# A two-block transformer on one core: memory keys ahead of the neighbourhood output product, and the modulation steps in another place

## The chip, the cores and the metric

The kernel runs on one core of one Trainium2 chip. The metric is device time in microseconds (us) of one execution. Before the change three runs gave 3050.26, 3059.8 and 3065.61 us; their median, 3059.8 us, is the number that the change is measured against.

## What is computed

The first block takes 512 tokens of 1024 features, normalizes them to `h` and projects them by one wide matrix `w_in`. Three branches follow, each gated by a sigmoid of its own part of that projection:

```python
rq, rk, rv, rg, nq, nk, nv, xq, gate_logits = jnp.split(h @ w_in[l], split_points, axis=-1)
y_ret = _retention_branch(rq, rk, rv, rg, ...)                          # 4 heads, decay both ways, group norm
y_na = _neighbourhood_attention(nq, nk, nv, na_rpb[l]) @ w_na_o[l]      # 8 heads, 8 x 16 windows
y_xa = _memory_cross_attention(xq, _rmsnorm(mem, g_mem[l]), w_mem_kv[l]) @ w_xa_o[l]   # 4 heads, 256 rows
x = x + (g_ret * y_ret + g_na * y_na + g_xa * y_xa) @ w_out[l]
x = x + _hierarchical_moe(...)
```

The second block is two layers of attention and feed-forward, whose norms are modulated by vectors that depend on one condition row alone:

```python
mod = (silu_c @ w_ada[l] + b_ada[l])[:, None, :]      # 1024 x 6144, two layers: 48 MB of weights
```

This last product, called `ada` in the kernel, needs nothing from the first block. The kernel computes it in small steps beside the first block's work.

## The kernel before

**Products.** A float32 product is three products of rounded halves, hi·hi, lo·hi and hi·lo (`mm3`, lines 99 to 101). Weights come in chunks of 1 MB, [128, 2048]. A chunk is loaded into a place called `raw` by a DMA on SyncE's queue (line 70), copied to `whi` by ScalarE (line 81), and `wlo` is the difference, made by VectorE (line 82). There are three places for each of `raw`, `whi` and `wlo`. `W` makes a pair where it is needed, `ahead` makes it earlier.

**The modulation in steps.** `ada()` is a generator of 48 steps. A step loads 1 MB of `w_ada` into a `raw` place (line 1299) and multiplies it by the condition on TensorE, four products with 32 rows of output (line 1301). Every eighth step ends a part: ScalarE copies the sums to `adar` (line 1305), TensorE turns them by four 128x128 products, VectorE copies them to `mod` (line 1310); the next part begins with the bias, `b_ada`, which also takes a `raw` place (lines 1294 and 1296). The sums lie in one bank of PSUM that is used again by every part. `bg(n)` takes n steps.

**Stages of the first block**, with the time at which each ends in the trace: retention with its gates (222 us), its output product `branch_out` (316), neighbourhood projections (391), neighbourhood heads (450), output product of two groups of columns (485), memory keys and values (518), output product of the other two groups (553), projection of the memory queries (577), memory heads (610), output product (685), then `w_out`, the router and the experts.

- `retention` (stages `queries`, `values`, `scores` for two pairs of heads, then four gate projections, then the transposed rows `yTh`, `yTl` from line 94 and 95). `proj_b` makes each projection of 256 columns and ends with one `bg()` step.
- `na_table`, in the retention, writes the table of position biases to DRAM, `rpb_d`, by 16 DMAs of 192 KB on the Pool engine's queue (line 536).
- `branch_out` has four groups of 256 columns, each with a gate chunk of `w_in` through `proj_a` and then the `bo` product; before group 2 of the neighbourhood's it calls `memory_keys`.
- `pairs` runs an attention as a pipeline over pairs of query tiles: scores `xs` or `ns`, exponentials, turned probabilities `prt`, values `xpo` or `npo`. It takes one `bg()` step per two pairs of the neighbourhood's 16, and one per pair of the memory's 8.

**What sets the order.** A scheduler at build time puts every instruction into a fixed order on its engine and gives out places of a pool as they come free. At run time an engine waits at the head of its list. A load that needs a `raw` place waits on SyncE's queue until the last reader of that place is done, and later loads of that queue wait behind it.

Of the kernel before, what the change touches and what calls it, by code (L numbers as in the profile page):

```python
# [8 lines left out]
F = mybir.dt.float32  # L9
# [3 lines left out]
OP = mybir.AluOpType  # L13
# [10 lines left out]
# columns of the vector pack, in blocks of 128 features  # L24
# [8 lines left out]
# groups of 256 columns of the second block's input projection: name, first column  # L33
# [4 lines left out]
class Kern:  # L38
    def __init__(self, tc, ins, outs, stop=None):
        self.tc = tc  # L40
        self.nc = tc.nc
        self.i = ins
        self.o = outs
        self.stop = stop
        self.es = ExitStack()
        self.early = {}

# [6 lines left out]
    def W(self, ap, n=2048, k=None, steps=1, pin=False, eng=None):  # L54
        """Weight chunk [128, n] of float32 from DRAM as an exact pair of float32r tiles."""
        key = ap.tensor.name, ap.offset
        if key in self.early:
            return self.early.pop(key)
        return self.pair(self.raw(ap, n), n, k, steps, pin, eng)

    def ahead(self, *chunks):
        """Loads weight chunks (name, index, k) before their use; W finds them then."""
# [10 lines left out]
    def pair(self, raw, n=2048, k=None, steps=1, pin=False, eng=None):  # L73
        """pin: not before what the engines have to do first, though it may seem ready."""
# [12 lines left out]
    def split(self, hi, lo, src, scale=None, bias=None):  # L87
        """hi + lo = src (times scale), both float32r."""
# [15 lines left out]
    def psum(self, mm, big=0, words=1024, own=()):  # L104
        """Banks of PSUM: mm of one bank, big of several."""
# [16 lines left out]
    def rows6(self, name, dtype=F):  # L122
        """[128, 6, 1024]: six tiles of rows, or what else takes their place."""
        return self.yp.tile([128, 6, 1024], dtype, name=name, tag="rows", bufs=1)
# [12 lines left out]
    def bcast_rows(self, ap, n, parts=128):  # L137
        """DRAM row of n elements seen by all partitions."""
        return bass.AP(tensor=ap.tensor, offset=ap.offset, ap=[[0, parts], [1, n]])

    def rinv(self, ss, n, count, eps, name):
        """1/sqrt(ss/count + eps) for a [128, n] tile: a first guess from the bits of the float, three Newton steps.
        With -r for the guess, (v r^2 - 3) r is 2 of the next one, and so on: -1, 2, -16, 8192 of them; v is 8192^2 of its own."""
# [33 lines left out]
    def transpose_rows(self, rows, nt, dst, evac):  # L177
        """rows: list of [128, 1024] tiles; evac(kt, t0, n, psum [128, n*128])."""
# [25 lines left out]
    # =====================================================================  # L204
# [30 lines left out]
    def b1_norm(self):  # L235
        """Loads the rows and the first weights; first_norm(t) and first_turn(t) then make the part of h of tile t."""
        nc = self.nc
        # products of nothing, that start the tensor engine's clock
# [36 lines left out]
    def first_norm(self, t):  # L275
        """Norms the row tiles from t on that share a step: 0, 1, or 2 and 3."""
# [23 lines left out]
    def w_in(self, g):  # L300
        """Columns 256*g.. of w_in, all of K."""
        return self.W(self.i["w_in"][g, 0], k=8)

    def proj_b(self, g, evac, after=lambda t: None, before=()):
        """Tokens on partitions: out[tok, 256 columns of group g]."""
# [10 lines left out]
        self.bg()  # L316

    def proj_a(self, g, evac):
        """Columns on partitions: out[128 columns, 512 tokens]."""
# [17 lines left out]
    def retention(self):  # L337
# [6 lines left out]
        y = rp.tile([128, 4, 1024], F, name="y")              # [tok, tile, 4 heads of 256]  # L344
# [3 lines left out]
        def queries(c):  # L348
            """q and k of the heads 2c, 2c + 1: [128, hi or lo, head, tok]"""
# [34 lines left out]
        def scores(hd):  # L384
            # decay by the distance of the tokens: E[p, i - 128 j + 384] for tile j of the keys
# [15 lines left out]
        def outputs(hd):  # L401
# [4 lines left out]
            for i in range(4):  # L406
# [6 lines left out]
                # group norm over the head's 256 values  # L413
# [9 lines left out]
        # log sigmoid of the decays: min(x, 0) - log1p(exp(-|x|)), log1p by its atanh series  # L423
# [23 lines left out]
        nc.sync.dma_start(diff, self.i["posdiff"])  # L447
        values(0)
# [16 lines left out]
        # silu of the gate projection  # L465
        for j in range(4):
# [7 lines left out]
            self.proj_b(8 + j, evac)  # L474
        yT = [[self.s8("yTh", [4, 512]) for _ in range(2)], [self.s8("yTl", [4, 512]) for _ in range(2)]]
# [11 lines left out]
    def branch_rows(self):  # L487
        """Where the rows of an attention branch are collected: [tok, tile, 512]."""
        return self.mix[:, 4:6].rearrange("p a (b c) -> p (a b) c", b=2)

    def branch_out(self, yT, nk, wname, gate_group, first=False, middle=lambda: None):
        """mix^T += sigmoid(gate^T) * (w^T y^T), features on partitions."""
        nc = self.nc
        nw = 2048 // nk                       # columns of w per chunk
        w = None
        for g in range(4):
            if g == 2:
                middle()
            if g * 256 % nw == 0:
                w = self.W(self.i[wname][g * 256 // nw, 0], k=nk)  # L500

            def evac(f, p, g=g, w=w):
                mx = self.mixT[:, 2 * g + f]
                gt = self.t5("gate")
                nc.scalar.activation(gt, p, AF.Tanh, scale=0.5)
                nc.vector.tensor_scalar(gt, gt, 1.0, 0.5, op0=OP.add, op1=OP.mult)
                py = self.mm("bo")
# [9 lines left out]
            self.proj_a(gate_group + g, evac)  # L517

# [1 line left out]
    def na_table(self):  # L520
        nc = self.nc
        # relative position bias, expanded: E[qr, h, x, kr] = rpb[h, kr - qr + 7, x - 16], x = kc - qc + 31
# [7 lines left out]
        # per query column qq of a tile, the 32 columns of its key window, for the three tile types  # L530
        # (window starts 16, 8 and 0 columns before the tile): [qq, qr, h, type, 256]
# [6 lines left out]
    def neighbourhood(self):  # L538
# [5 lines left out]
        T = {}  # L544
# [13 lines left out]
        starts = (256, 192, 64, 0)               # key windows of the query tiles 3, 2, 1, 0  # L558
# [34 lines left out]
        self.pairs(16, scores, values, ("w_na_o", (0, 0), 4), ("w_in", (24, 0), 8), ("w_in", (25, 0), 8))  # L593
# [4 lines left out]
        oT = self.rows_to_T(o[:, ::-1])  # L598
        self.branch_out(oT, 4, "w_na_o", 24, middle=lambda: self.memory_keys(rows))

    def exps(self, out, s, m, scale):
        """out = exp(scale * (s - max)) for two tiles of queries [128, 2, 256]; returns 1 / row sums."""
# [10 lines left out]
    def pairs(self, n, scores, values, *chunks):  # L613
        """n pairs of query tiles: scores(i) -> probabilities [128, 2, 256], 1 / sums; values(i, turned, 1 / sums);
        chunks: weights that are needed next."""
# [3 lines left out]
        for i in range(n + 1):  # L619
# [17 lines left out]
            if i % 2 or n == 8:  # L637
                self.bg()
# [11 lines left out]
    def memory_rows(self):  # L650
        """Normed rows of the memory."""
# [14 lines left out]
    def memory_keys(self, rows):  # L666
        """Keys and values of the memory."""
# [25 lines left out]
    def memory_attention(self):  # L693
# [29 lines left out]
        self.pairs(8, scores, values, ("w_xa_o", (0, 0), 4), ("w_in", (28, 0), 8), ("w_in", (29, 0), 8))  # L723
# [7 lines left out]
    def b1_out(self, *stages):  # L731
        """stages: what follows for each tile of rows; the sums of squares of its parts are in self.xss."""
# [39 lines left out]
    # =====================================================================  # L772
    def moe(self):
# [21 lines left out]
        # normed rows, to DRAM for the gathers and transposed for the router  # L795
# [37 lines left out]
        # group: maximum of the softmax, first one on ties  # L833
# [45 lines left out]
        # slots: rank of the token among those of its expert, 512 slots per expert  # L879
# [20 lines left out]
        for k, w in ((0, w1), (1, w2)):  # L900
            # rank r and first slot 512 e of the token's k-th expert
# [10 lines left out]
            # the last expert's rows are not gathered  # L912
# [13 lines left out]
            # the rest: slot 512 e + r - CAP  # L926
# [1325 lines left out]
```

## Time and profile before

| what | value |
| --- | --- |
| runs | 3050.26, 3059.8, 3065.61 us, median 3059.8 |
| span of the profiled execution (its own time is not listed apart from the span) | 3055.9 us |
| median less span | 3.9 us |
| TensorE busy | 2907.7 us, 95% |
| VectorE, ScalarE, Pool busy | 1784.5, 1296.3, 483.3 us |
| DMA | 399.78 MB, 131 GB/s over the span |

TensorE is busy nearly all the time, so what can change is where it waits, and how long it runs at the lower of its two clocks after it has waited. The granted clock is given as a share of the full 2.4 GHz: 0.50 is 1.2 GHz. A wait is listed with what ended it. Line numbers are those of the kernel before; in the kernel after, lines past the first few are moved by one or more (the load is line 71, the split 82 and 83, the products 100 to 102, the modulation's load 1322 and product 1324).

### The profile page before, as it was taken

To read this page: it belongs to the slowest core of one execution; us is meant where nothing else is said; L and a number is where in the kernel's file an instruction comes from. 1 tells how busy PE (TensorE), PEld (TensorE's weight loads), DVE (VectorE), ACT (ScalarE), POOL (GpSimd) and SP (SyncE) were. 2 spreads that over 40 slices of the span, in tenths; PEclk is the share of its full clock that TensorE was granted. 3 is DMA by queue.
4 is the path that set the end of the run, shared out by engine and by line. 5 is a ranking of instruction groups with operands and counts; after the bars stand their busy time and mean duration, and the time that the engine had idled before them with its cause. 6 is when DMAs were issued, how large, how long until landed. Compare 5 with 4: busy or idle time off the path is not lost. (4 is left out here: it accounts for less than half of the span.)

```text
span 3055.9 us, 44719 instructions
## 1 busy us (share of the span) xinstructions
PE 2907.7 (95%) x17896; PEld 2473.1 (81%) x17896; DVE 1784.5 (58%) x3187; ACT 1296.3 (42%) x2275; POOL 483.3 (16%) x478
## 2 busy tenths in 40 slices
PE   8999999999899979899998999999898999899998
PEld 6997777679788869787688888888798776788887
DVE  6652254346688876788747242434665886644445
ACT  3232243324577754597645121211342876432222
POOL 2200010001110042255312000000310543100001
PEclk9999999999899989999999999999999999899999
DMA  5443464446799862510023121212143300322221
GB/s 197 153 140 138 143 234 152 183 155 242 267 392 378 312 225 75 179 27 19 1 90 128 59 71 54 78 48 83 62 138 98 96 20 1 125 110 96 97 97 69
DMA packets 130084, 399.78 MB, mean 131 GB/s; under 512 B 62199, under 2 KB 74887, under 8 KB 93128
## 3 DMA queue, kind: packets, MB, share of 16 engines
q1 hardware_dynamic: 116206, 350.04, 31.9%
q0 software_dynamic: 13520, 46.55, 4.6%
q8 instruction: 143, 2.34, 0.3%
q14 instruction: 71, 0.58, 0.1%
q10 hardware_dynamic: 144, 0.26, 0.0%
HBM read 356.64 MB, written 39.39 MB: 130 GB/s over the span
## 5 line engine op out<-in xcount | busy, mean ns | idle before, releaser
L82 DVE TENSOR_TENSOR wlo<-raw,whi 128x2048 fp32r<-128x2048 f32 (+2 forms) x195 | 419.3, 2153 | 280.2 <-ACT whi L81 279.7
L81 ACT ACTIVATE whi<-raw 128x2048 fp32r<-128x2048 f32 (+2 forms) x203 | 351.9, 1739 | 490.9 <-PE fd L101 132.2
L99 PE MATMUL fg<-hT,whi 128*128 128x512 f32 (+1 forms) x1120 | 389.1, 348 | 2.1 <-ACT hT L1374 2.1
L100 PE MATMUL fg<-hT,whi 128*128 128x512 f32 (+1 forms) x1120 | 389.7, 348 | 1.2 <-POOL hT L1376 1.2
L101 PE MATMUL fg<-hT,wlo 128*128 128x512 f32 (+1 forms) x1120 | 389.2, 348 | 0.0
L100 PEld LDWEIGHTS fg<-hT,whi 128*128 128x128 f32 x1120 | 213.7, 191 | 31.0 <-POOL hT L1376 1.7
L99 PEld LDWEIGHTS fg<-hT,whi 128*128 128x128 f32 x1120 | 212.1, 190 | 31.9 <-ACT hT L1374 2.5
L101 PEld LDWEIGHTS fg<-hT,wlo 128*128 128x128 f32 x1120 | 212.0, 189 | 29.0
L1942 POOL TENSOR_TENSOR pelo<-pe,pehi 128x512 fp32r<-128x512 f32 x140 | 180.7, 1292 | 233.5 <-DVE pehi L1941 227.1
L2104 DVE TENSOR_TENSOR sg<-sg,fg 128x512 f32<-128x512 f32 (+1 forms) x70 | 40.1, 572 | 295.0 <-PE fg L101 295.0
L101 PE MATMUL fd<-whi,hl 128*128 128x512 f32 x440 | 174.9, 397 | 0.0
L1905 DVE TENSOR_REDUCE smx<-sn 128x1 f32<-128x768 f32 x160 | 152.3, 952 | 38.2 <-PE sn L1899 37.7
L100 PE MATMUL fd<-wlo,hh 128*128 128x512 f32 x440 | 174.6, 397 | 0.0
L99 PE MATMUL fd<-whi,hh 128*128 128x512 f32 x440 | 174.1, 396 | 0.0
L2080 POOL TENSOR_TENSOR acc<-acc,gt 128x512 f32<-128x512 f32 x20 | 30.7, 1536 | 867.9 <-ACT sqj L164 867.9
L2075 DVE TENSOR_TENSOR acc<-acc,fd 128x512 f32<-128x512 f32 x180 | 120.7, 685 | 71.9 <-PE fd L101 71.9
L131 PE MATMUL tp<-ident,pn 128*128 128x128 f32 x960 | 151.8, 278 | 2.6 <-DVE pelo L92 1.8
L1908 ACT ACTIVATE pn<-sn,smx 128x768 f32<-128x768 f32 x160 | 143.5, 902 | 12.0 <-DVE smx L1905 6.8
L99 PE MATMUL eg<-whi,xt 128*96 128x256 f32 x512 | 146.5, 286 | 0.0
L100 PE MATMUL eg<-wlo,xt 128*96 128x256 f32 x512 | 144.6, 282 | 0.9 <-DVE wlo L82 0.9
L82 DVE TENSOR_TENSOR wlo<-rawx,whi 128x2048 fp32r<-128x2048 f32 x58 | 132.9, 2292 | 20.9 <-ACT whi L81 20.8
L101 PE MATMUL eg<-whi,xt 128*96 128x256 f32 x512 | 144.3, 282 | 0.0
(661 smaller groups left out, 7755.8 us busy)
## 6 DMA issues: line engine op xcount, KB each, us to landing
raw<-in_w_in SPq DMA_DIRECT2D x53, 1024.0 KB, 5.0
raw<-in_w_ada SPq DMA_DIRECT2D x48, 1024.0 KB, 5.1
raw<-in_f_gate SPq DMA_DIRECT2D x22, 1024.0 KB, 4.8
raw<-in_f_up SPq DMA_DIRECT2D x22, 1024.0 KB, 4.8
raw<-in_f_down SPq DMA_DIRECT2D x22, 1024.0 KB, 4.8
rawx<-in_e_gate SPq DMA_DIRECT2D x19, 1024.0 KB, 14.2
rawx<-in_e_up SPq DMA_DIRECT2D x19, 1024.0 KB, 8.9
rawx<-in_e_down SPq DMA_DIRECT2D x18, 1024.0 KB, 8.3
```

Of the source, the lines that this page charges most:

```text
L81: keep(nc.scalar.activation(hi[:, c], raw[:, c], AF.Copy))
L82: keep((eng or nc.vector).tensor_tensor(lo[:, c], raw[:, c], hi[:, c].bitcast(F), op=OP.subtract))
L99: t.matmul(ps, lh, rh, start=first, stop=False)
L100: t.matmul(ps, lh, rl, start=False, stop=False)
L101: t.matmul(ps, ll, rh, start=False, stop=last)
L131: self.nc.tensor.transpose(out, in_, self.ident[:k, :k])
L1905: nc.vector.tensor_reduce(m[:, t:t + 1], p[:, :768], axis=AX.X, op=OP.max, negate=True)
L1908: nc.scalar.activation(P[t], p[:, :768], AF.Exp, bias=m[:, t:t + 1], accum_out=su[:, t:t + 1])
L1942: nc.gpsimd.tensor_tensor(el, e, eh.bitcast(F), op=OP.subtract)
L2075: nc.vector.tensor_tensor(acc[:, t, cs], acc[:, t, cs], p, op=OP.add)
L2080: nc.gpsimd.tensor_tensor(acc[:, t, cs], acc[:, t, cs], gt[t // 4][:, cs], op=OP.mult)
L2104: nc.vector.tensor_tensor(sg, sg, pp[1], op=OP.mult)
```

## The change

It has four parts.

1. `proj_b` takes `self.steps` modulation steps instead of one. `self.steps` is 2 from `values(0)` of the retention to its last gate, else 1.
2. `branch_out` becomes a loop over a generator, `branch_steps`, with two stops for each half of a group: one behind the gate, one behind the output product. The next gate chunk is asked for by `ahead` in the second half of the group.
3. After the neighbourhood heads, `memory_keys` comes at once. The neighbourhood's `branch_steps` is kept, and the memory heads advance it: two stops per pair. The rest follows behind the heads. The heads themselves take no modulation step of their own any more; one is taken at the end of each group of `branch_steps`.
4. The weight chunks that the heads ask for ahead change with that: the three first chunks of `w_mem_kv` in the neighbourhood heads, none in the memory heads, where `w_xa_o` and the first gate chunk follow behind the pipeline.

```diff
         self.skew(4, *before, product, after)
-        self.bg()
+        self.bg(self.steps)
...
         nc.sync.dma_start(diff, self.i["posdiff"])
+        self.steps = 2
         values(0)
...
             self.proj_b(8 + j, evac)
+        self.steps = 1
...
+    def branch_steps(self, yT, nk, wname, gate_group, first=False):
...
         for g in range(4):
-            if g == 2:
-                middle()
             if g * 256 % nw == 0:
                 w = self.W(self.i[wname][g * 256 // nw, 0], k=nk)
-
-            def evac(f, p, g=g, w=w):
-                mx = self.mixT[:, 2 * g + f]
+            wg = self.w_in(gate_group + g)
+            for f in range(2):
+                p = self.mm("prj")
...
                 nc.vector.tensor_scalar(gt, gt, 1.0, 0.5, op0=OP.add, op1=OP.mult)
+                yield
+                if f == 1 and g < 3:
+                    self.ahead(("w_in", (gate_group + g + 1, 0), 8))
...
-            self.proj_a(gate_group + g, evac)
+                yield
+            self.bg()
...
-        self.pairs(16, scores, values, ("w_na_o", (0, 0), 4), ("w_in", (24, 0), 8), ("w_in", (25, 0), 8))
+        def beside(i):
+            if i % 2:
+                self.bg()
+
+        self.pairs(16, scores, values, beside, ("w_mem_kv", (0, 0), 8), ("w_mem_kv", (1, 0), 8), ("w_mem_kv", (2, 0), 8))
...
-        oT = self.rows_to_T(o[:, ::-1])
-        self.branch_out(oT, 4, "w_na_o", 24, middle=lambda: self.memory_keys(rows))
+        self.na_out = self.branch_steps(self.rows_to_T(o[:, ::-1]), 4, "w_na_o", 24)
+        self.memory_keys(rows)
...
-            if i % 2 or n == 8:
-                self.bg()
+            beside(i)
...
-        self.pairs(8, scores, values, ("w_xa_o", (0, 0), 4), ("w_in", (28, 0), 8), ("w_in", (29, 0), 8))
+        def beside(i):
+            for _ in range(2):
+                next(self.na_out, None)
+
+        self.pairs(8, scores, values, beside)
+        for _ in self.na_out:
+            pass
+        self.ahead(("w_xa_o", (0, 0), 4), ("w_in", (28, 0), 8))
```

The rest of the diff takes comments out. Each engine has the same instructions as before, in another order; from the end of the memory branch's output product on, the order is the same.

**Loads at the third gate projection (end of the retention).** SyncE's queue before; `raw_2190` holds the weights of the third gate, `raw_2178` the bias of a new modulation part:

```order
L70 DMA raw_2051<-in_w_in 128x2048
L1294 DMA raw_2178<-in_b_ada 1x2048
L1299 DMA raw_2184<-in_w_ada 128x2048
L70 DMA raw_2190<-in_w_in 128x2048
L1299 DMA raw_2316<-in_w_ada 128x2048
L70 DMA raw_2322<-in_w_in 128x2048
```

The same queue now; `raw_2100` and `raw_2260` are the weights of the second and the third gate:

```order
L71 DMA raw_2100<-in_w_in 128x2048
L1322 DMA raw_2226<-in_w_ada 128x2048
L1317 DMA raw_2248<-in_b_ada 1x2048
L1322 DMA raw_2254<-in_w_ada 128x2048
L71 DMA raw_2260<-in_w_in 128x2048
L1322 DMA raw_2386<-in_w_ada 128x2048
L1322 DMA raw_2392<-in_w_ada 128x2048
L71 DMA raw_2398<-in_w_in 128x2048
```

Two steps and a bias, so three places, now stand between two gates' weights; `raw_2260` gets the place of `raw_2226`. TensorE's list there before, from the end of the second gate's product:

```order
L101 MATMUL prj_2147<-whi_2053,hTl_119 128x256
L1296 MATMUL ada_2177<-raw_2178,ones2_393 32x512 x4
L1301 MATMUL ada_2177<-raw_2184,silu_c_390 32x512 x4
L99 MATMUL prj_2196<-whi_2192,hTh_116 128x256
L100 MATMUL prj_2196<-wlo_2193,hTh_116 128x256
```

And now:

```order
L102 MATMUL prj_2196<-whi_2102,hTl_119 128x256
L1324 MATMUL ada_1382<-raw_2226,silu_c_390 32x512 x4
L132 MATMUL ada_2234<-ident_90,adar_2232 128x128 x4
L1319 MATMUL ada_2247<-raw_2248,ones2_393 32x512 x4
L1324 MATMUL ada_2247<-raw_2254,silu_c_390 32x512 x4
L100 MATMUL prj_2266<-whi_2262,hTh_116 128x256
L100 MATMUL prj_2296<-whi_2262,hTh_116 128x256
L100 MATMUL prj_2326<-whi_2262,hTh_116 128x256
L100 MATMUL prj_2356<-whi_2262,hTh_116 128x256
L1324 MATMUL ada_2247<-raw_2386,silu_c_390 32x512
L101 MATMUL prj_2266<-wlo_2263,hTh_116 128x256
```

The reader of `raw_2226` stands directly ahead of the gate that uses `raw_2260`, with the turn of a part, a bias and one step between them.

**ScalarE at the transposed rows of the retention.** Before, `whi_2521` is the first chunk of `w_ret_o`, `whi_2527` the first gate chunk of the output product (two of eight `yTh` rows are shown):

```order
L81 ACTIVATE whi_2521<-raw_2519 128x2048
L470 ACTIVATE th_2353<-prj_2328 128x256
L81 ACTIVATE whi_2527<-raw_2525 128x2048
L470 ACTIVATE th_2383<-prj_2358 128x256
...
L94 ACTIVATE yTh_2454<-trp_2458,vecs_92 128x512
...
L94 ACTIVATE yTh_2455<-trp_2507,vecs_92 128x512
L81 ACTIVATE whi_2647<-raw_2645 128x2048
```

Now `whi_2603` and `whi_2609` are these two chunks:

```order
L82 ACTIVATE whi_2603<-raw_2601 128x2048
L472 ACTIVATE th_2489<-prj_2464 128x256
L472 ACTIVATE th_2519<-prj_2494 128x256
L95 ACTIVATE yTh_2536<-trp_2540,vecs_92 128x512
...
L95 ACTIVATE yTh_2537<-trp_2589,vecs_92 128x512
L82 ACTIVATE whi_2609<-raw_2607 128x2048
L82 ACTIVATE whi_2697<-raw_2695 128x2048
```

The gate chunk's copy has moved from ahead of the eight `yTh` copies to behind them.

**TensorE in the memory heads.** Before, one pair of tiles:

```order
L101 MATMUL xs<-mk,xql 128x256
L131 MATMUL prt<-ident,xpr 128x128 x4
L1301 MATMUL ada<-raw,silu_c 32x512 x3
L719 MATMUL xpo<-mv,prT 128x128 x4
L1301 MATMUL ada<-raw,silu_c 32x512
L99 MATMUL xs<-mk,xqh 128x256
```

Now (`prj` and `bo` are the neighbourhood's gate and output products, 24 and 12 instructions for one pair):

```order
L102 MATMUL xs<-mk,xql 128x256
L132 MATMUL prt<-ident,xpr 128x128 x4
L735 MATMUL xpo<-mv,prT 128x128 x4
L100 MATMUL prj<-hTh,whi 128x512
L101 MATMUL prj<-hTl,whi 128x512
L102 MATMUL prj<-hTh,wlo 128x512
```

In place of a modulation step, half a group of the neighbourhood's output now lies between two pairs of the memory heads.

## Rows read from the trace of the kernel before

**Rows 1.** The page's part 1: span, then TensorE's busy us, share, count.

```profile
span 3055.9 us, 44719 instructions
...
PE 2907.7 (95%) x17896; PEld 2473.1 (81%) x17896; DVE 1784.5 (58%) x3187; ACT 1296.3 (42%) x2275; POOL 483.3 (16%) x478
```

**Rows 2.** Waits of TensorE, 391 to 685 us: total us, times, longest.

```profile
PE ada L1301 <- DMA raw<-in_w_ada: 3.7, 2, 3.5
PE ns L99 <- DVE smx L578: 1.9, 2, 1.8
PE mvp L100 <- DVE wlo L82: 1.5, 1, 1.5
PE prt L131 <- ACT nsc L608: 1.1, 1, 1.1
```

**Rows 3.** Stretches: length, busy PE, PEld, DVE, ACT, POOL, clock, DMA, GB/s.

```profile
599.50:603.00 3.50, 0.07 (x1) 0.00 (x0) 2.36 (x3) 1.81 (x6) 0.00 (x0) 0.88 0.98 401
...
603.00:605.00 2.00, 1.91 (x9) 0.24 (x9) 0.00 (x0) 0.00 (x0) 0.00 (x0) 0.50 0.17 68
...
607.00:608.90 1.90, 1.90 (x11) 1.90 (x10) 0.42 (x1) 0.97 (x2) 0.00 (x0) 0.50 0.90 366
...
442.00:445.00 3.00, 3.00 (x17) 1.83 (x10) 1.32 (x4) 0.60 (x1) 1.81 (x4) 0.50 1.00 344
```

**Rows 4.** Timeline, a gate stage: start, busy us, engine, line, [idle before].

```profile
181.04 1.06 PE L1301 MATMUL ada<-raw,silu_c 128*32 128x512 f32 x6
...
183.20 0.60 PE L131 MATMUL ada<-ident,adar 128*128 128x128 f32 x4
...
182.15 0.33 SPq L70 DMA_DIRECT2D raw<-in_w_in  x1
...
186.99 1.92 ACT L81 ACTIVATE whi<-raw 128x2048 fp32r<-128x2048 f32 x1 [0.97 <-DMA raw<-in_w_in]
...
188.94 2.29 DVE L82 TENSOR_TENSOR wlo<-raw,whi 128x2048 fp32r<-128x2048 f32 x1 [2.00 <-ACT whi L81]
```

**Rows 5.** Timeline, end of the retention rows' gates and start of their product.

```profile
221.55 3.71 PE L131 MATMUL trp<-ident,y 128*128 128x128 f32 x32
...
225.02 0.48 PE L99 MATMUL prj<-hTh,whi 128*128 128x512 f32 x1
...
222.24 4.73 ACT L94 ACTIVATE yTh<-trp,vecs 128x512 fp32r<-128x512 f32 x8 [1.20 <-PE trp L131]
...
226.82 1.97 ACT L81 ACTIVATE whi<-raw 128x2048 fp32r<-128x2048 f32 x1
```

**Rows 6.** Issues; then queues (packets, MB, share), twice 90:94, once 94:98.

```profile
80.93 7.28 POOL L536 DMA_DIRECT2D rpb_d<-rpbe  x12 [18.95 <-DVE rpbe L529]
...
88.50 0.33 SPq L1299 DMA_DIRECT2D raw<-in_w_ada  x1
...
q0 software_dynamic: 245, 0.75, 96.7%
...
q1 hardware_dynamic: 6, 0.05, 2.9%
...
q1 hardware_dynamic: 117, 0.89, 60.4%
```

**Rows 7.** Timeline, queries of the second pair of heads.

```profile
93.39 0.69 DVE L92 TENSOR_TENSOR rp<-pf,rp 128x512 fp32r<-128x512 f32 x1
...
97.17 1.21 POOL L364 TENSOR_TENSOR rp<-rp,rp 128x256 f32<-128x256 f32 x1 [4.75 <-DVE gn_t L158]
...
98.33 1.91 PE L1301 MATMUL ada<-raw,silu_c 128*32 128x512 f32 x12
```

**Rows 8.** Timeline, end of the neighbourhood heads; one load in the memory heads.

```profile
449.78 1.92 PE L131 MATMUL trp<-ident,mix 128*128 128x128 f32 x16
...
454.83 1.42 DVE L663 TENSOR_SCALAR xr<-xr,mem_y 128x1024 f32<-128x1024 f32 x2
...
593.99 0.33 SPq L1299 DMA_DIRECT2D raw<-in_w_ada  x1
```

More of the change, by code (lines that the diff above doesn't have):

```diff
@@ L474, in retention @@
             self.proj_b(8 + j, evac)
+        self.steps = 1
         yT = [[self.s8("yTh", [4, 512]) for _ in range(2)], [self.s8("yTl", [4, 512]) for _ in range(2)]]
@@ L489, in branch_rows, with branch_out @@
         return self.mix[:, 4:6].rearrange("p a (b c) -> p (a b) c", b=2)
-    def branch_out(self, yT, nk, wname, gate_group, first=False, middle=lambda: None):
+    def branch_out(self, *args, **more):
+        for _ in self.branch_steps(*args, **more):
+            pass
+    def branch_steps(self, yT, nk, wname, gate_group, first=False):
         nc = self.nc
@@ L496, in branch_out @@
         for g in range(4):
-            if g == 2:
-                middle()
             if g * 256 % nw == 0:
                 w = self.W(self.i[wname][g * 256 // nw, 0], k=nk)
-            def evac(f, p, g=g, w=w):
-                mx = self.mixT[:, 2 * g + f]
+            wg = self.w_in(gate_group + g)
+            for f in range(2):
+                p = self.mm("prj")
+                fs = slice(f * 128, f * 128 + 128)
+                for kt in range(8):
+                    self.mm3(p, wg[0][:, kt, fs], wg[1][:, kt, fs], self.h(0, kt), self.h(1, kt), kt == 0, kt == 7)
                 gt = self.t5("gate")
@@ L506, in evac @@
                 nc.vector.tensor_scalar(gt, gt, 1.0, 0.5, op0=OP.add, op1=OP.mult)
+                yield
+                if f == 1 and g < 3:
+                    self.ahead(("w_in", (gate_group + g + 1, 0), 8))
+                mx = self.mixT[:, 2 * g + f]
                 py = self.mm("bo")
@@ L611, in exps, with pairs @@
         return rec
-    def pairs(self, n, scores, values, *chunks):
+    def pairs(self, n, scores, values, beside, *chunks):
         nc = self.nc
@@ L721, in values @@
                                     rec[:, :, None].to_broadcast([128, 2, 128]), op=OP.mult)
-        self.pairs(8, scores, values, ("w_xa_o", (0, 0), 4), ("w_in", (28, 0), 8), ("w_in", (29, 0), 8))
+        def beside(i):
[3 more added lines that the diff above has]
+        for _ in self.na_out:
+            pass
+        self.ahead(("w_xa_o", (0, 0), 4), ("w_in", (28, 0), 8))
         if self.stop == "xa":
```

## The prediction

> **What bounds the kernel now.** I read the page's first part, then the waits of TensorE, the stretches around the longest of them, and the timelines of the stages that the change touches. TensorE is busy 2907.7 of 3055.9 us [rows 1], so a stage costs what its products cost plus what TensorE waits in it. Between 391 and 685 us, where most of the edited code lies, the listed waits are 3.7 us for a modulation load, 1.9 and 1.1 us in the neighbourhood heads, and 1.5 us for the low half of a chunk of the memory values: 8.2 us of 294 [rows 2]. A wait costs more than its length. From 599.5 to 603.0 TensorE did 0.07 us of work, and afterwards its granted clock was 0.50, the lower level of 1.2 GHz, until about 608.9 [rows 3]. Work done at half the clock takes twice as long, so those 5.9 us held 2.95 us of full-speed work: 2.95 us lost besides the 3.43. In the neighbourhood heads a shorter wait is followed by 0.50 over 442 to 445 [rows 3]; with its edges I count 3.4 us, so 1.7 lost.
>
> So little can be won here: even all of it, 8.2 + 2.95 + 1.7, is 12.9 us, 0.4% of the time. What decides is whether the new order makes new waits elsewhere. I therefore went through the new order for every load, split and product between 20 and 685 us, with durations from the trace.
>
> **What goes.** (1) In the memory heads the modulation steps, one per pair, wanted weights faster than they came: a load issued at 593.99 [rows 8] was still waited for at 603.0 [rows 3]. Now half a group of output product, 24 + 12 products of 512 columns, lies between pairs, and the steps there are four, not nine. The wait and its slow stretch go: 3.43 + 2.95 = 6.4 us (bounds 0 and 6.6). (2) The wait of 1.5 us in the memory values [rows 2] goes, since their chunks are asked for in the heads before (bounds 0 and 1.5). (3) In the neighbourhood heads chunks are still split among the softmax work, others than before; of the present 1.9 + 1.1 + 1.7 = 4.7 us I take 0.8 as gone (bounds: 4.7 gone, or 2 more). Together 8.7 us.
>
> **What comes: one load that is late.** At the third gate the weights `raw_2260` take the place of the modulation weights `raw_2226`, and the reader of those stands directly ahead of the gate in TensorE's list. The chain from that reader's end to the split weights is in the trace in another gate stage: the step that begins at 181.04 ends at 182.10, the load is issued at 182.15, its copy starts at 186.99 and the low half ends at 188.94 + 2.29 = 191.23 [rows 4]. That is 9.1 us. TensorE has little to do meanwhile. The four turned products wait for the copy of the sums and end 1.7 us behind the reader (183.20 + 0.60 - 182.10 [rows 4]); then bias and one step, 2.1 us by the 1.06 of a step [rows 4]; later four first passes and one modulation product, 0.75 us as an estimate. So 1.7 - 0.6 = 1.1 us idle before the turn, and 9.1 - 1.7 - 2.1 - 0.75 = 4.6 us behind: 5.7 us. With the slow stretch after the one wait of like size, 2.95, that makes 8.65 us. Bounds: 0, if something else covers it; 12.8, if the landing takes the 9 us of the load at 593.99. I take the value between, as that stage's DMA traffic is nearest to the stage measured. Queued behind this load on SyncE's queue are the loads of the fourth gate, which then come late by the same, but so does the work before them.
>
> **A split behind eight copies.** At the turned rows of the retention the first gate chunk's copy has moved behind the eight `yTh` copies in ScalarE's list. In the trace before, TensorE turns the rows from 221.55 and begins the gate's products at 225.02, 3.47 us later, without a wait. The eight copies run from 222.24 for 4.73 us, and the next copy of weights ends at 226.82 + 1.97 = 228.79 [rows 5]. In the new order the gate needs that copy: 228.79 - 225.02 = 3.8 us of idle, and 2.95 for the clock: 6.75 us (bounds 0 and 9). The low half is ready soon enough, as nine products of the output stand ahead of it.
>
> **A load among the table's writes.** In the retention, two steps per projection put the key weights of the second pair of heads behind two modulation loads. Their places come free at about 84.7 and 85.7 us (estimate, the end of the modulation products behind the pair's values). By then the Pool engine is issuing the bias table's writes: 12 of 192 KB from 80.93, one per 0.607 us [rows 6]. What a load does there is shown once: one issued at 88.50 had moved nothing to speak of by 94, 6 packets against 245 of the writes, which moved 0.75 MB in 4 us; then the loads' queue moved 0.89 MB in 60.4% of 4 us [rows 6]. So loads seem to be served in the order of issue. Ahead of ours are 8 writes, 1.5 MB, of which 0.9 are done by 85.7 at 0.19 MB per us; the rest takes 3.3 us, to 89.0; two loads at 0.89 / 2.42 = 0.37 MB per us take 5.7, to 94.7; copy and low half 1.92 + 2.29 and their starts, to about 99.2. On VectorE that low half stands ahead of work that now begins at 93.39 and ends with the Pool engine's sum of 97.17 + 1.21 [rows 7]; without one product of 0.7 that moved ahead, 4.3 us. So the sum is ready at 103.5 to 104, where TensorE arrives at 98.33 + 1.91 = 100.24 [rows 7]. Wait 3.8, clock 2.95: 6.75 us (bounds 0; 15, if the load lies behind all the writes).
>
> By the Trainium skill, page "DMA: Bandwidth & Descriptors", section "Queues, rings and completion order", each DMA engine goes round among the queue rows that have work, packet by packet. By that rule our load would not wait behind the writes but share with them; with packets of 0.89 MB / 117 against 0.75 MB / 245 [rows 6] it would get some 70%, and this term would be about 4 us, the time 3073. The row of 90 to 94 us, 6 packets against 245, speaks against the rule here.
>
> **Memory keys without cover.** The memory's rows are normed until 454.83 + 1.42 = 456.25 [rows 8]. Before, the first two groups of output product covered that. Now the keys follow the turned heads (449.78 + 1.92 = 451.70 [rows 8]) with a step, the turn of a part and a bias, some 3 us, between. TensorE stands for about 1.4 us, and for the sums' copy and the `mod` copy of the part's end some 0.9: 2.3 us (bounds 0 and 5.5). At the start of the memory heads a gate chunk's copy stands ahead of softmax work: 0.5 us.
>
> **The sum.** New waits 8.65 + 6.75 + 6.75 + 2.3 + 0.5 = 24.95; gone 8.7; net 16.2 us. On the profiled execution that is 3055.9 + 16.2 = 3072.1, and with the 3.9 us by which the median of the runs lies above its span, 3076.0. The products are the same in kind and number, so nothing else changes.
>
> **Rivals.** *Only the planned gap.* The load at the third gate is late and the memory keys wait, but the turned rows and the table's writes are covered, because the copies or the loads come a little earlier than the trace before suggests: 8.65 + 2.3 + 0.5 - 8.7 = +2.75, 3062.5. For it: both terms rest on 3.8 us of idle, and a shift of TensorE by an earlier wait gives just that much room. Against: nothing ahead of them in the retention shifts TensorE alone.
> *Not slower: the loads come before they are needed.* If the third gate's place is free one reader earlier, the load is issued some 11 us earlier, behind the second gate's products, and the other splits follow in time; then only the memory keys' wait stands against the gains: 2.8 - 8.7 = -5.9, 3053.9, and with the whole 4.7 of the neighbourhood heads 3050. It decides from a load issue 5.7 us ahead of the reader's end. Against: in SyncE's list two steps and a bias lie between two gates, and there are three places.
> *Worse: the queue is full.* Twice the modulation loads run in the retention. If they land after 8 to 9 us, as at 593.99, and the key weights lie behind all the writes, the third term is up to 15 and the first 12.8, and one more gate waits: 10 to 18 more, about 3090. For it: order of issue in rows 6. Against: the retention's traffic has room elsewhere.
>
> **Numbers.** What a measurement here can tell from no change is about 0.5%, 15.3 us: faster is below 3044.5, slower above 3075.1. Chances: forecast 0.45 (its own range 3067 to 3086, half and a little more of it slower), only the gap 0.17 (no change), not slower 0.18 (0.08 of it faster), worse 0.20 (slower). So faster 0.08, same 0.43, slower 0.49. Range 3053 to 3094; it takes in most of the lower rivals and the upper one.
>
> **What would show it.** In the profile after: a wait of TensorE near 210 us of `prj` for `whi` at a gate, 3 us and then 1 to 2 for `wlo`; one near 245 us of `prj` for `whi` behind `yTh`; one near 105 us of `rpt` for the Pool engine; each followed by a clock of 0.50. No wait for modulation loads in the memory heads, and a clock of 1.00 there. The retention would end some 33 us later, 10.6 by its ten more steps of 1.06 us and the rest by waits. I am wrong if these waits come to less than 10 us, or if waits appear in the memory heads that I did not count.

## The result: slower by 0.85%

Five runs of the changed kernel gave 3078.0 to 3089.12 us, median 3082.29; the kernel before, in the same session, 3050.26 to 3065.61, median 3059.8. The ratio of the times is 1.0085, 95% interval 1.0062 to 1.0108, so 19 to 33 us slower. The forecast was 3076.0, within 3053 to 3094.

The page's part 1 of the profile after, which answers to [rows 1]:

```profile
span 3076.3 us, 44716 instructions
...
PE 2914.0 (95%) x17896; PEld 2480.9 (81%) x17896; DVE 1782.9 (58%) x3187; ACT 1298.8 (42%) x2275; POOL 483.6 (16%) x478
```

The span is 20.4 us longer. TensorE's busy time hardly differs, so the rest is waiting and slow work. Four stretches of the first block show where. They are cut at TensorE's first instruction of the turned retention rows, of the neighbourhood heads, of the turned rows of the heads, and of the first block's last turned rows. The columns are length, then busy us (and count) of PE, PEld, DVE, ACT, POOL, the mean granted clock of TensorE, DMA share and GB/s. Before:

```profile
20.00:221.55 201.55, 196.29 (x1547) 179.10 (x1546) 127.15 (x298) 58.36 (x89) 31.06 (x46) 1.00 0.44 149
221.55:392.20 170.65, 170.65 (x896) 136.23 (x892) 48.28 (x48) 40.05 (x45) 2.74 (x6) 1.00 0.39 140
392.20:449.80 57.60, 54.59 (x369) 37.36 (x366) 33.37 (x126) 33.01 (x87) 9.39 (x18) 0.97 0.71 243
449.80:708.60 258.80, 253.58 (x1431) 200.14 (x1430) 111.40 (x178) 81.27 (x134) 7.73 (x15) 0.99 0.49 180
708.60:3055.90 2347.30, 2220.68 (x13635) 1913.80 (x13634) 1451.72 (x2485) 1073.55 (x1905) 426.52 (x384) 0.97 0.34 119
```

After:

```profile
20.00:258.90 238.90, 220.82 (x1641) 191.42 (x1639) 127.64 (x302) 57.75 (x89) 33.04 (x50) 0.93 0.45 160
258.90:435.00 176.10, 172.53 (x896) 137.35 (x892) 50.72 (x50) 41.95 (x46) 2.71 (x6) 0.99 0.40 144
435.00:496.80 61.80, 61.10 (x369) 42.91 (x366) 32.53 (x124) 33.63 (x88) 8.37 (x16) 0.86 0.71 253
496.80:737.80 241.00, 238.89 (x1338) 198.20 (x1337) 108.65 (x175) 80.66 (x131) 6.73 (x13) 0.99 0.41 147
737.80:3076.30 2338.50, 2209.18 (x13634) 1904.96 (x13634) 1451.17 (x2485) 1075.08 (x1905) 426.89 (x384) 0.97 0.34 119
```

| stretch | before | after | difference |
| --- | --- | --- | --- |
| retention | 201.55 | 238.90 | +37.35 |
| its output product, neighbourhood projections | 170.65 | 176.10 | +5.45 |
| neighbourhood heads | 57.60 | 61.80 | +4.20 |
| memory keys to the end of the first block | 258.80 | 241.00 | -17.80 |
| everything later | 2347.30 | 2338.50 | -8.80 |

The first block lost 29.2 us. Ten modulation steps of 1.06 us moved from the fourth stretch into the first, and with them the bias (1.06 us) and the turn (0.60 us) of one part: of the 94 products that the first stretch has more, these are 80, 8 and 4. That is 12.3 us of work, which comes off the first difference and is added to the fourth: 25.0 us lost in the retention, and 5.5 gained behind the heads. The last row is the same program in the same order; it is taken up at the end.

The waits of TensorE that are new, from its timeline (start, busy us, instruction; in brackets the idle time before it and what ended it):

```profile
61.46 0.44 PE L132 MATMUL rpt<-ident,rp 128*128 128x128 f32 x2 [2.07 <-POOL rp L365]
...
111.52 0.69 PE L132 MATMUL rpt<-ident,rp 128*128 128x128 f32 x2 [3.96 <-POOL rp L365]
...
136.31 0.44 PE L132 MATMUL rpt<-ident,rp 128*128 128x128 f32 x2 [1.56 <-POOL rp L365]
...
137.70 0.69 PE L132 MATMUL ada<-ident,adar 128*128 128x128 f32 x2 [0.96 <-ACT adar L1328]
...
222.33 0.66 PE L132 MATMUL ada<-ident,adar 128*128 128x128 f32 x4 [0.72 <-ACT adar L1328]
...
223.27 1.06 PE L1319 MATMUL ada<-raw,ones 1*32 1x512 f32 x8 [0.28 <-DVE mod L1333]
...
228.50 1.22 PE L100 MATMUL prj<-whi,hTh 128*128 128x256 f32 x4 [3.17 <-ACT whi L82]
...
266.17 0.50 PE L100 MATMUL prj<-hTh,whi 128*128 128x512 f32 x1 [3.57 <-ACT whi L82]
...
478.99 0.58 PE L100 MATMUL ns<-nkh,nqh 64*128 64x256 f32 x1 [0.53 <-DVE smx L591]
...
499.29 1.06 PE L1324 MATMUL ada<-raw,silu_c 128*32 128x512 f32 x8 [0.59 <-DMA raw<-in_w_ada]
...
501.13 0.66 PE L132 MATMUL ada<-ident,adar 128*128 128x128 f32 x4 [0.78 <-ACT adar L1328]
...
503.71 1.54 PE L132 MATMUL trp<-ident,xr 128*128 128x128 f32 x6 [0.42 <-DVE xr L679]
```

And the granted clock behind some of them, in stretches (columns as above):

```profile
112.00:118.00 6.00, 6.00 (x33) 6.00 (x33) 4.48 (x11) 0.83 (x3) 1.11 (x1) 0.57 0.01 1
138.00:148.00 10.00, 10.00 (x46) 6.45 (x45) 1.39 (x6) 0.38 (x1) 0.00 (x0) 0.51 0.56 212
228.50:233.00 4.50, 4.50 (x12) 2.56 (x13) 2.28 (x1) 0.00 (x0) 0.00 (x0) 0.50 0.82 303
480.00:496.00 16.00, 16.00 (x72) 11.87 (x72) 7.20 (x19) 7.75 (x16) 4.73 (x9) 0.50 0.59 201
502.50:509.00 6.50, 6.08 (x25) 3.30 (x18) 5.84 (x13) 2.67 (x7) 1.01 (x2) 0.53 0.79 299
545.00:647.00 102.00, 102.00 (x541) 81.95 (x534) 40.67 (x66) 34.05 (x61) 1.54 (x3) 1.00 0.35 124
```

The third gate's weights are waited for at 228.50, the gate chunk behind the `yTh` copies at 266.17, the rotary sum of the second pair of heads at 111.52: the three waits of the forecast, 3.17, 3.57 and 3.96 us long, with a clock of 0.50 to 0.57 over the microseconds behind the first and the last of them. The rows at 61.46, 136.31 and 137.70 were not in it. In the memory heads the clock is 1.00 (they lie within 545 to 647 us) and no modulation load is waited for: the 3.7 us of [rows 2] are gone, and so are the 1.5 us of `mvp`.

### The profile page after: what moved, and what is told of

The parts are those of the page before. It is cut to its first block, busy times and chain, and to the rows that moved or that the text cites. A ratio compares the mean times of both kernels' runs of the same rounds, so it can differ in the third digit from the quotient of the medians.

```text
span 3076.3 us, 44716 instructions
## 1 busy us (share of the span) xinstructions
PE 2914.0 (95%) x17896; PEld 2480.9 (81%) x17896; DVE 1782.9 (58%) x3187; ACT 1298.8 (42%) x2275; POOL 483.6 (16%) x478
```

## The experiments

The theory: the doubled steps cause nearly all of the loss, because a second modulation load in every projection delays the next weights, and their split then stands in the way of other work on VectorE and ScalarE. The order of the branches by itself gains. Rivals: the order of the branches costs; or the DMA traffic as such, in whatever order; or the bias table's writes alone.

**The steps taken back.**

```diff
-        self.steps = 2
+        self.steps = 1
         values(0)
...
             for _ in range(2):
                 next(self.na_out, None)
+            self.bg()
```

> The change without its doubled modulation steps: one step per projection in the retention as before, and one step per pair in the memory heads, beside the output product. In the profiles of before and after, the first block's last turned rows begin at 708.6 and 737.8 us, 29.2 apart; the retention up to its turned rows accounts for 37.3 of it, of which some 10.6 are the added steps' own work. Theory (the loss is the waits that the doubled steps make in the retention; the rest of the change gains): the retention is as before, its turned rows begin at 221 to 224, no wait for whi at a gate or behind yTh, and the time is 2 to 9 us below before, ratio 0.997 to 0.999. Rival (modulation loads in the memory heads are late whatever lies beside them): TensorE waits there for w_ada again, 3 us or more with a slow stretch, and the ratio is 1.000 to 1.003. Second rival (the loss is in the keys ahead of the output product, or in the other chunks that the neighbourhood heads split): ratio 1.004 or more, with the first block still over 12 us behind.

Measured: ratio 1.0025 (1.0008 to 1.0042), 3063.53 us against 3055.85. One wait, and three stretches, the retention, the neighbourhood heads and what follows them to the end of the block, in this kernel's profile:

```profile
636.39 0.79 PE L100 MATMUL prj<-hTh,whi 128*128 128x512 f32 x1 [5.75 <-ACT whi L82]
...
20.00:225.40 205.40, 200.00 (x1549) 182.98 (x1547) 127.91 (x301) 59.33 (x90) 31.07 (x46) 0.97 0.43 147
...
396.40:470.80 74.40, 72.50 (x369) 48.47 (x366) 33.62 (x126) 33.72 (x88) 9.37 (x18) 0.70 0.57 195
...
470.80:730.90 260.10, 251.68 (x1430) 200.58 (x1429) 111.80 (x178) 81.71 (x133) 7.73 (x15) 0.98 0.48 177
```

The retention is back at 205.4 us, and neither gate wait is left, as the theory has it. But the ratio is the first rival's, though not by its place: the wait is 5.75 us for the first gate chunk of the last output product. Its load is issued only at 627.94 us, behind six modulation loads that SyncE's queue issued from 590 to 616. The last stretch, 260.1 us, gains nothing on the 258.8 before, so with nine steps still in the memory heads the order of the branches gains nothing, against the theory. The neighbourhood heads' stretch was also 17 us longer in this execution, which took 3077.76 us, at a clock of 0.70; that is no part of the edit: the run of six steps, below, has the same neighbourhood heads, and takes 60.1 us for them.

**The doubled steps alone**, on the kernel before.

```diff
-        self.bg()
+        self.bg(getattr(self, "steps", 1))
...
+        self.steps = 2
         values(0)
...
             self.proj_b(8 + j, evac)
+        self.steps = 1
```

> The kernel before with the doubled modulation steps of the retention alone; the order of the branches is the old one, and the memory heads find no steps left to take. Theory: the retention is as slow as after the change, its turned rows near 259 us, and as the memory heads lose their late loads (3.5 us and 3 for the clock) but also their filler, the whole is 20 to 36 us above before, ratio 1.007 to 1.012. Rival (the branches' order is what costs): the retention is slower only by the steps' own 10.6 us, its turned rows before 240, and the ratio is 0.998 to 1.002.

Measured: 1.0088 (1.0055 to 1.012). Retention, the stretch from the turned rows of the neighbourhood heads to the end of the block, and the longest group of TensorE's waits in that stretch (total us, times, longest):

```profile
20.00:255.50 235.50, 218.00 (x1637) 188.57 (x1636) 127.07 (x299) 57.18 (x88) 33.00 (x50) 0.95 0.46 162
...
489.40:731.50 242.10, 235.21 (x1339) 195.87 (x1337) 110.84 (x175) 80.76 (x134) 7.72 (x15) 1.00 0.41 150
...
PE xpo L721 <- ACT prT L632: 4.3, 4, 1.6
```

This part alone loses as much as the whole change (1.0085), as the theory has it. The retention is 34 us longer than before. The last stretch is 16.7 us shorter: 12.3 are the steps that went, with their bias and turn. The late loads in the memory heads are gone too; in their place came 5.4 us of waits for ScalarE's softmax work, 4.3 of them in the line shown. So the interleaving is not needed to lose the wait for the late loads; taking steps out of the heads does it too. Nor does the order of the branches gain anything that shows: with the same steps in it, the last stretch takes 242.1 us in the old order, 241.0 after the change, and 242.4 in the next run, which has the changed order. The new order loses the softmax waits, but pays for the memory keys, 2.07 us of waits and some 3 us at the low clock of 502.5 to 509 us.

**The next weights asked for ahead of the two steps, at the gates.**

```diff
         self.skew(4, *before, product, after)
+        self.ahead(*then)
         self.bg(self.steps)
...
-            self.proj_b(8 + j, evac)
+            self.proj_b(8 + j, evac, then=[("w_in", (9 + j, 0), 8)] if j < 3 else [("w_ret_o", (0, 0), 8), ("w_in", (20, 0), 8)])
```

> The change, with each gate's following chunk asked for before the two modulation steps instead of behind them, and so the first two chunks of the output product. Only the order of loads and splits at the four gates changes. Theory (the load at the third gate is late for want of a place, and the copy behind the yTh copies is late by its place in the list): the waits of 3.17 us at the gate and of 3.57 us behind yTh go, with their slow stretches; 10 to 14 us less than after, ratio to before 1.003 to 1.006. Rival (two modulation loads per projection are too much for the DMA, so the loads are late in any order): both waits stay or move to the modulation products, and the ratio stays 1.007 to 1.010.

Measured: 1.004 (1.0017 to 1.0063). Retention, output product with projections, and the last stretch:

```profile
20.00:251.80 231.80, 217.40 (x1634) 190.32 (x1633) 129.41 (x297) 58.81 (x90) 32.91 (x50) 0.94 0.48 171
...
251.80:423.20 171.40, 170.68 (x896) 136.26 (x892) 48.48 (x49) 39.90 (x45) 2.71 (x6) 1.00 0.37 138
...
482.30:724.70 242.40, 238.82 (x1338) 197.78 (x1336) 108.68 (x175) 81.21 (x133) 6.71 (x13) 0.99 0.41 149
```

7.1 us gone from the first and 4.7 from the second, and no wait for `whi` in either; the ratio is in the theory's range. The same traffic in another order, so for these two waits the order was it, not the amount. The rotary waits of the retention stay.

**Doubled steps at the gates only**, the other six in the memory heads.

```diff
-        self.steps = 2
         values(0)
...
+        self.steps = 2
         for j in range(4):
...
                 next(self.na_out, None)
+            self.bg()
```

> The change with doubled modulation steps at the four gates only; the six steps that values and queries took are taken one per pair in the memory heads. Theory: the waits of TensorE for the rotary sums near 61, 111 and 136 us and their slow stretches go, some 18 to 22 us, while the gate's and the yTh copy's waits stay: ratio to before 1.002 to 1.005. Rival (the queries were late by the table's writes alone, as I forecast, 6.75 us): only the wait near 111 us goes, and the ratio is 1.005 to 1.007.

Measured: 1.007 (1.0052 to 1.0089), above the theory's numbers and at the upper end of the rival's. The retention and the last stretch:

```profile
20.00:235.50 215.50, 206.24 (x1578) 185.01 (x1577) 125.76 (x297) 57.20 (x88) 31.44 (x47) 0.96 0.43 148
...
476.00:729.00 253.00, 248.13 (x1395) 198.88 (x1394) 110.57 (x175) 81.51 (x134) 7.73 (x15) 0.98 0.47 171
```

The retention is 23.4 us shorter than after the change; six steps with a bias and a turn are 8.1 of it, so some 15 us of waits and slow work went with the steps of values and queries: far more than the 6.75 of the rival. Of the waits for rotary sums none is longer than before: those near 61, 111 and 136 us are all gone, as the theory has it, and not the one near 111 alone. But the last stretch is 12 us longer, and only 7.4 of that are steps; TensorE now waits 2.18 us there for a modulation load and 1.98 for the memory's rows. I had counted the steps as free where they went. They are not.

**Six steps in the memory heads, the rest in the last output product**: the run with the steps taken back, with `if i < 6:` ahead of its `self.bg()`, and

```diff
                 yield
-            self.bg()
+            self.bg(self.steps)
...
+        self.steps = 2
         self.branch_out(oT, 4, "w_xa_o", 28)
+        self.steps = 1
```

> As the run with the doubled steps taken back, but the memory heads take six modulation steps, not nine, and the last output product of the block takes two per group instead, so that the first chunks of that product are asked for before the last modulation loads. In the earlier run TensorE waited 5.75 us for the copy of its first gate chunk at 636 us, with a slow stretch behind it. Theory (this wait is a load that stands behind modulation loads in SyncE's queue): it goes, 6 to 9 us less than that run, ratio to before 0.998 to 1.001. Rival (the modulation steps make such a wait wherever they stand): a wait of like size appears in the last output product, for whi or for w_ada, and the ratio stays 1.002 to 1.004.

Measured: 0.9973 (0.9948 to 0.9997), 3050.07 us against 3057.91. Retention, heads, last stretch:

```profile
20.00:224.70 204.70, 198.92 (x1546) 181.94 (x1545) 127.34 (x297) 58.64 (x90) 31.04 (x46) 0.98 0.44 147
...
395.80:455.90 60.10, 57.08 (x369) 39.35 (x366) 33.37 (x126) 33.59 (x88) 9.34 (x18) 0.91 0.71 252
...
455.90:707.30 251.40, 248.54 (x1430) 199.43 (x1429) 111.17 (x178) 81.63 (x133) 7.72 (x15) 0.99 0.49 181
```

The wait is gone, and this version is faster than the kernel before, by 1 to 16 us: just clear of the noise, and a little better than the theory's numbers. Against the run with the steps taken back the ratios differ by 0.0052, some 16 us, about twice the 6 to 9 forecast; the last stretch accounts for 8.7 of it, and the rest is not accounted for. The last stretch is 7.4 us shorter than before, with as many steps in it. The run with the steps taken back has the same order of branches and gained nothing there, so the 7.4 us are what that order and the new places of the steps are worth together. The retention's 3.2 us more lie ahead of its first scores.

**The next weights first at every projection of the retention.**

```diff
+        nxt = {4: 5, 5: 1, 1: 3, 3: 6, 6: 7, 7: 8}.get(g) if self.steps == 2 else None
+        self.ahead(*(then or ([] if nxt is None else [("w_in", (nxt, 0), 8)])))
         self.bg(self.steps)
```

> The change, doubled steps and all, with the next chunk asked for before the two modulation steps at every projection of the retention from the first values on, not at the gates alone. Theory (the doubled steps cost because each pair of them pushes the next weights back in the queue and their split into the middle of other work): the waits for the rotary sums near 61, 111 and 136 us go as well, the turned rows begin at 234 to 242 us (258.9 after the change, 251.8 with the gates' loads first), and the ratio to before is 0.998 to 1.002. Rival (the split of the values and keys lands in the rotary products' way whatever the order of loads, or the table's writes hold the loads): over 5 us of waits for the rotary sums stay, turned rows later than 246 us, ratio 1.003 or more.

Measured: 1.0034 (1.0011 to 1.0058). Issue of the key weights and their copy; issue and copy of the chunk that follows them, the weights of the next values (told apart by the order of the loads); and one of the waits:

```profile
66.43 0.33 SPq L71 DMA_DIRECT2D raw<-in_w_in  x1
...
75.89 1.91 ACT L82 ACTIVATE whi<-raw 128x2048 fp32r<-128x2048 f32 x1
...
91.75 1.41 SPq L71 DMA_DIRECT2D raw<-in_w_in  x1
...
104.33 1.92 ACT L82 ACTIVATE whi<-raw 128x2048 fp32r<-128x2048 f32 x1 [5.73 <-DMA raw<-in_w_in]
...
112.40 0.69 PE L132 MATMUL rpt<-ident,rp 128*128 128x128 f32 x2 [4.15 <-POOL rp L367]
```

The rival's outcome in the ratio and in the waits: rotary waits of 2.40, 4.15 and 1.62 us stay, and the turned rows begin at 253.0. The edit did bring the key weights early: they are issued at 66.43 and copied at 75.89, where after the change it was 91.07 and 103.45. But the next chunk now takes their place among the table's writes. It needs 12.6 us from issue to copy, its low half stands ahead of the same rotary products on VectorE, from 106.28 to 108.57, and the wait is there as before. Asking sooner moved the late load on to the next chunk; it did not make the place come free among fewer writes.

**The table's writes later.**

```diff
-        self.na_table()
...
         scores(3)
+        self.na_table()
         outputs(3)
```

> The change, with the position table's writes to DRAM (16 of 192 KB on the Pool engine's queue) moved from behind the first scores to behind the last scores of the retention; nothing else. In the trace after the change the load of the second pair's key weights is issued at about 92 us among these writes, its copy begins at 103.45, and TensorE waits 3.96 us for the rotary sum at 111.5 with a slow stretch behind. Theory (the load waits for the writes issued before it): without them it lands 5 to 7 us after its issue, by 99, its low half is done by 103, and the wait at 111 us goes (0 to 0.5 us); the waits near 61 and 136 us and at the third gate stay; 5 to 8 us less than after, ratio to before 1.005 to 1.007. Rival (the three places and the order of the splits hold it, not the writes): the copy begins 10 us or more after the issue again, and the wait stays over 3 us.

Measured: 1.0079 (1.0056 to 1.0102). The interval holds most of the theory's range and also the 1.0085 of no change; the profile decides. Issue, copy, and the retention:

```profile
92.45 0.33 SPq L71 DMA_DIRECT2D raw<-in_w_in  x1
...
99.22 1.90 ACT L82 ACTIVATE whi<-raw 128x2048 fp32r<-128x2048 f32 x1
...
20.00:254.50 234.50, 220.00 (x1640) 191.46 (x1638) 127.77 (x302) 57.69 (x89) 33.21 (x50) 0.93 0.49 166
```

Issue to copy is now 6.8 us instead of 12.4, and the wait at 111 us is gone; the retention is 4.4 us shorter. So the writes had held that load for 5.6 us, which is more than the wait. The waits near 61 and 131 us and at the third gate stay. The 4.4 us are less than the 5 to 8 forecast, and less than the wait with its slow stretch; where the rest went was not followed.

## Why the prediction was right, and where it was short

The direction and its cause were right: doubled steps alone give 1.0088, the change 1.0085. That the number came so near has luck in it. The forecast was 16.2 us more; the span grew by 20.4, but only because the unchanged rest ran 8.8 us faster in this execution, and the first block itself lost 29.2. By stretches, forecast and found: retention 15.4 and 25.0, product 6.75 and 5.45, neighbourhood heads -0.8 and +4.2, the rest of the block -5.1 and -5.5. By the forecast's own steps:

- *What goes, and the memory keys.* 6.4 + 1.5 us less 2.8 of new waits, 5.1 net, were forecast behind the neighbourhood heads; the last stretch gained 5.5. Of the new waits the memory keys' came to 0.59 + 0.78 + 0.28 + 0.42 = 2.07 us, 2.3 forecast. Right, but the clock of 0.53 from 502.5 to 509 us, some 3 us more, was not in the sum. The 0.8 in the neighbourhood heads failed: the two waits of 3.0 us shrank to 0.7, but the stretch is 4.2 us longer, with a clock of 0.50 from 480 to 496 us instead of the 3 us of [rows 3]. That the change causes this is not shown: the run with the loads first at the gates has the same order in the heads and takes 59.1 us for them, against 57.6 before and 61.8 after.
- *The third gate.* Forecast 5.7 us idle and 2.95 for the clock, found 0.72 + 0.28 + 3.17 = 4.17 us and half of 4.5 us at 0.50, 2.25. Mechanism right, size a third too large. The chain itself was right: the reader ends at 221.61, and the low half at 230.77, 9.16 us later. But the four first passes and the modulation product, put at 0.75 us, took from 228.50 to 231.55 at the half clock and hid the wait for `wlo`. Asking for the load earlier took the wait away.
- *The split behind eight copies.* 3.8 us of idle forecast, 3.57 found; 6.75 with the clock, and the whole stretch, in which nothing else changed much, is 5.45 longer, so the clock cost 1.9 and not 2.95. Right.
- *The load among the writes.* Forecast: issue 85.7, low half done 99.2, wait 3.8. The wait of 3.96 is right, but not by the forecast's steps: issue came 5.4 us later than forecast, the low half 8.5, and TensorE itself arrived at 107.56, 7.3 us later than the 100.24 of the sum, as it had waited and done more steps by then. The two delays nearly cancel, which is luck:

```profile
91.07 1.51 SPq L71 DMA_DIRECT2D raw<-in_w_in  x1
...
103.45 1.92 ACT L82 ACTIVATE whi<-raw 128x2048 fp32r<-128x2048 f32 x1 [5.54 <-DMA raw<-in_w_in]
...
105.40 2.29 DVE L83 TENSOR_TENSOR wlo<-raw,whi 128x2048 fp32r<-128x2048 f32 x1 [4.42 <-ACT whi L82]
```

Copy 12.4 us behind the issue, low half done at 107.69, rotary sum from 110.74 to 111.46. The writes (q0) and the loads (q1) in the DMA queues meanwhile (packets, MB, share of the engines; two rows for 90 to 94 us, then two for 94 to 101):

```profile
q0 software_dynamic: 232, 0.72, 94.1%
...
q1 hardware_dynamic: 9, 0.07, 4.4%
...
q1 hardware_dynamic: 248, 1.89, 71.8%
q0 software_dynamic: 253, 0.77, 29.1%
```

For the first microseconds the loads' queue moves 9 packets against 232, as in [rows 6]. The modulation load ahead of ours was issued at 90.2, and its first packets come behind 93, when some 7 of the 8 or 9 writes issued before it are done. So far the order of issue, as I read it, fits. From then on it does not: from 94 to 101 the two queues move 248 and 253 packets, one for one, although some of the writes were issued behind our load. [rows 6] has the like, which I left out: in the trace before, the writes' queue still moved 167 packets from 94 to 98 us beside the 117 of the loads. So the loads shared with the writes once they had begun, and the two took some 8 us where 5.7 was forecast. The Trainium skill's page "DMA: Bandwidth & Descriptors", section "Queues, rings and completion order", has the DMA engines take turns between queues, packet by packet. From 94 us on this case's trace agrees: the loads got 71% of the bytes, the 70% that I worked out for that rule. In the microseconds before it does not.

- *What was missed*, and why the loss is 29 us in the first block and not the 16.2 of the sum: the rotary waits at 61.46 and 136.31 and the part's end at 137.70, 2.07 + 1.56 + 0.96 us, with 10 us at a clock of 0.51 behind the last. With 0.42 us at 51 us and 1.7 for the clock behind 61 they come to some 11.6 us. The third gate, 6.4, and the key weights, 3.96 and some 2.6 for the clock, make 13 more, so nearly all of the retention's 25.0 is named. The step that failed is the walk through the new order in the rotary stages: there I checked loads against products, but not where each split now stands among the rotary multiplications of VectorE, nor that a part of the modulation now ends among them. The run with doubled steps at the gates only, in which these waits are absent, shows that the steps cause them.

## What to carry to other kernels

Work that fills gaps is not free where its loads share places with others: here, with three places in one queue, a second background load per projection made the next weights, or their split, late at five points of the retention and its product. Ask for what the critical engine reads next ahead of the background's loads, and read from the order what stands between a place's last reader and its next; here 12 us came back by that at the gates, and nothing more by doing it at the other projections, where the next chunk took the late place. And judge a change of order part by part: here the doubled steps account for the loss, the new order of the branches shows no gain by itself, and 7 us were gained only where the steps, too, stood where nothing waited behind their loads.

## What the runs showed of the hardware

Two things lie beside the kernels. In the neighbourhood heads the low clock came and went with the execution: it held from 480 to 496 us after the change, behind a wait of only 0.53 us, and in the profiled execution of the run with the steps taken back most of the stage ran at it, 41 us at 0.50 from 423 to 464 us. TensorE counts as busy there for 40.45 us, but with 155 products in them. In most of these kernels longer times go with a lower clock over the whole execution: of the six-step kernel, 3046.6 us at 0.975 and 3072.1 at 0.965; of the kernel before, 3047.5 at 0.977 and 3081.1 at 0.968. So a single profile of these kernels says little about 10 us; the same stage of several does.

The other: in the second block's first feed-forward, with a granted clock of 1.00 and the same order, TensorE did 523 products from 1800 to 1900 us of the profile before and 532 in the same 100 us after the change. From the first to the last product of its second matrix (`fd`) the stage took 498.2 us before and 491.1 after, which is 7.1 of the 8.8 us in the table. One other profile, that of the doubled steps at the gates, had the slower pace, 526, the others 531 to 535; no run here shows what sets it.
